# Attention value products of a small decoder trunk: from float32 products of one head each to split products of a head pair

## The chip, the cores and the metric

One core of one Trainium2 chip. The metric is the device time of one execution in microseconds; below it is the median of three runs. Five engines work side by side: TensorE (PE, matmuls; its weight loads are listed as PEld), VectorE (DVE), ScalarE (ACT), GpSimd (POOL) and SyncE (SP, which issues most transfers). Matmul results land in PSUM, eight banks of 512 float32 columns on 128 partitions; everything else lies in SBUF.

## The reference, cut to what matters

Two layers on a sequence of 256 tokens, width 1024, 16 heads of 64. Layer 0 has eight block-sparse heads and eight heads that attend to 64 keys selected by an indexer; layer 1 has sixteen dilated heads. At this length each head is a causal softmax with a bias, and then the product of the weights with the values:

```
p = jax.nn.softmax(logits, axis=-1).astype(v.dtype)
return (jnp.einsum('bhqnk,bhqnkd->bhqd', p_sel, v_sel)
        + jnp.einsum('bhqk,bhkd->bhqd', p_own, v_own))
...
x = x + mixed @ w_o[layer]
h = rmsnorm(x, ffn_norm[layer])
x = x + conv_ffn(h, w_up[layer], conv_w[layer], conv_b[layer], w_down[layer])
```

All is float32.

## The kernel before, in words

Nearly all products are made from exact parts: a float32 operand is split into a high part (a copy rounded to the type F32R by ACT) and a low part (operand minus high part, by DVE), and three products high x high, high x low, low x high are summed in PSUM (`mm3`, line 130). `split` (lines 121, 122) does this for a weight block of 128 x 1024 right before it is used; raw blocks have three buffers, parts have five.

Attention in either layer goes over four chunks of four heads. A chunk projects q and k (`proj_fm`, 256 columns each, result with features on partitions) and v (`proj_v`, result with tokens on partitions, evacuated by ACT on line 312 into the float32 tile V, which holds all 1024 value columns for both token tiles t = 0, 1). Then come two calls of `head_pair`, two heads s = 0, 1 each:

- `logits`: queries on partitions, keys in columns. Queries 0 to 127 see keys 0 to 127 (128 columns), queries 128 to 255 all 256, so a head has 384 columns (TW). Products on lines 357 and 358, into one of two PSUM banks "lg".
- DVE adds the bias and takes the minimum (line 375), ACT takes the exponential and its sum (378), DVE inverts the sums (380) and scales the 128 and the 256 columns (382).
- PE transposes the three 128-column blocks (385) into the one PSUM bank "pt", and ACT copies them to SBUF as float32 (387): keys 0 to 127 against 256 queries, then keys 128 to 255 against the last 128 queries.
- Value products are plain float32 products (lines 392 and 396): a head's 64 value columns are the stationary operand, so its result stands on 64 of the 128 partitions of the one PSUM bank "av", head 0 on the lower half, head 1 on the upper. The trace shows each float32 product as two records.
- ACT copies the result as high part `mxh` (397), DVE makes the low part `mxl` (398).

`out_proj` then sums the output projection over the eight pairs hp; pairs 0 to 4 may start early, 5 to 7 close each of the four PSUM banks in turn, after which a norm reads them and the FFN follows (up products line 130, tiles u; down products, tiles o). The last pair (hp 7) uses the banks in other roles.

In layer 0 DVE also selects keys between the projections: 16 rounds of maximum and replace on the scores (lines 696, 697), whose result `selb` is needed from head 8 on. POOL adds it to the bias there (lines 724, 725). The indexer runs ahead of the attention.

The order of instructions on every engine is fixed when the program is built: a planner goes by program order, priorities and estimated times, so products of the next chunk and of the output projection stand between those of a head pair. At run time each engine takes its instructions in that order. A tile with a tag shares its buffers with all tiles of that tag; a new one is written when the one before it in the buffer is no longer read.

## Time and profile before

| what | value |
|---|---|
| runs | 663.56, 663.67, 664.44 us; median 663.67 |
| profiled execution | 663.93 us, span from first to last instruction 662.1 us |
| granted TensorE clock | 0.997 of full |
| PE busy | 649.3 us, 98% of the span, 5145 products |
| DVE, ACT, POOL busy | 530.5, 406.2, 58.0 us (80%, 61%, 9%) |
| DMA | 116.01 MB, mean 175 GB/s |

Busy time is the time in which at least one instruction of an engine runs. Products on PE overlap in a pipeline, so what one costs is seen from the start of one to the start of the next, not from its duration. The share of an engine is a mean over stages: indexer to 66 us, layer 0's attention to 153 us, its FFN to 363 us, layer 1's attention to 458 us, and its FFN.

### The profile page before, as it was taken

What the parts mean: (1) busy time and instruction counts of PE and PEld (TensorE: products, weight loads), DVE (VectorE), ACT (ScalarE), POOL (GpSimd) and SP (SyncE); (2) the same over time, 40 slices, a digit from 0 to 9 for tenths busy, and PEclk for the clock granted to TensorE, in tenths of its full rate; (3) what the DMA queues carried; (4) which work ended last, traced back from release to release, by engine and by line L of the source; (5) the groups of instructions that cost most, each with busy time, mean ns of one, the idle gap of its engine ahead of it and who ended that gap; (6) DMA issues with size and microseconds to landing.
All of it is one profiled execution on the core that took longest, in us unless ns stands there. A gap on an engine that the chain in (4) does not pass through costs nothing.

```text
span 662.1 us, 12930 instructions
## 1 busy us (share of the span) xinstructions
PE 649.3 (98%) x5145; PEld 616.6 (93%) x5145; DVE 530.5 (80%) x1012; ACT 406.2 (61%) x710; POOL 58.0 (9%) x68
## 2 busy tenths in 40 slices
PE   8999999999999999999999999999999999999995
PEld 6999998988999999999989988999999999999994
DVE  5999998966898777777779977765999777777774
ACT  6766774765676555555546866764587555555553
POOL 0100001712100000000013111010300000000002
PEclk9999999999999999999999999999999999999998
DMA  9986644462766666666323534537366555555201
GB/s 272 292 243 188 174 137 153 157 220 98 247 216 207 208 207 207 207 207 207 128 65 128 192 101 155 191 128 256 117 184 227 195 186 185 184 185 187 105 1 63
DMA packets 91604, 116.01 MB, mean 175 GB/s; under 512 B 3447, under 2 KB 83191, under 8 KB 91544
## 3 DMA queue, kind: packets, MB, share of 16 engines
q1 hardware_dynamic: 86492, 110.09, 50.5%
q10 hardware_dynamic: 5052, 5.10, 3.3%
q8 instruction: 40, 0.66, 0.4%
q14 instruction: 20, 0.16, 0.1%
HBM read 113.35 MB, written 1.84 MB: 174 GB/s over the span
## 4 chain that ended last, share of the span: by engine, by line
PE 95%; DVE 2%; DMA 1%; issue 1%; SPq 0%; ACT 0%; POOL 0%; POOLq 0%; DVEq 0%
PE f0u L130 18%; PE f1u L130 18%; PE f1o L130 9%; PE f0o L130 9%; PE a0o L130 3%; PE a1o L130 3%; PE a0av L392 1%; PE a1av L392 1%; PE a_0pt L385 1%; PE v02p L130 1%; PE v11p L130 1%; PE v01p L130 1%; PE v12p L130 1%; PE v03p L130 1%; PE v13p L130 1%; PE k02p L130 1%
## 5 line engine op out<-in xcount | busy, mean ns | idle before, releaser
L130 PE MATMUL f0u<-f0xl,f0w_0h 128*128 128x256 f32 x176 | 49.5, 281 | 1.2 <-DVE f0xl L204 1.2
L130 PE MATMUL f1u<-f1xl,f1w_0h 128*128 128x256 f32 x176 | 49.5, 281 | 0.3
L130 PE MATMUL f0u<-f0xh,f0w_0l 128*128 128x256 f32 x176 | 49.2, 280 | 0.0
L130 PE MATMUL f1u<-f1xh,f1w_1h 128*128 128x256 f32 x176 | 49.2, 280 | 0.0
L130 PE MATMUL f0u<-f0xh,f0w_1l 128*128 128x256 f32 x176 | 49.1, 279 | 0.0
L130 PE MATMUL f1u<-f1xl,f1w_1h 128*128 128x256 f32 x176 | 49.1, 279 | 0.0
L130 PE MATMUL f1u<-f1xh,f1w_0l 128*128 128x256 f32 x176 | 49.1, 279 | 0.0
L130 PE MATMUL f0u<-f0xh,f0w_1h 128*128 128x256 f32 x176 | 49.1, 279 | 0.0
L130 PE MATMUL f0u<-f0xh,f0w_0h 128*128 128x256 f32 x176 | 49.1, 279 | 0.0
L130 PE MATMUL f0u<-f0xl,f0w_1h 128*128 128x256 f32 x176 | 49.1, 279 | 0.0
L130 PE MATMUL f1u<-f1xh,f1w_1l 128*128 128x256 f32 x176 | 49.1, 279 | 0.0
L130 PE MATMUL f1u<-f1xh,f1w_0h 128*128 128x256 f32 x176 | 49.1, 279 | 0.0
L523 DVE SCALAR_TENSOR_TENSOR f1c<-f1us,cv,f1c 128x255 f32<-128x255 f32 (+1 forms) x88 | 37.0, 475 | 0.7 <-ACT f1c L520 0.7
L523 DVE SCALAR_TENSOR_TENSOR f0c<-f0us,cv,f0c 128x255 f32<-128x255 f32 (+1 forms) x88 | 36.9, 476 | 0.0
L121 ACT ACTIVATE f1w_0h<-f1uv 128x1024 fp32r<-128x1024 f32 x22 | 23.2, 1056 | 21.9 <-PE f1u L130 21.9
L121 ACT ACTIVATE f0w_0h<-f0uv 128x1024 fp32r<-128x1024 f32 x22 | 23.3, 1057 | 21.8 <-PE f0u L130 21.5
L130 PEld LDWEIGHTS f0u<-f0xl,f0w_0h 128*128 128x128 f32 x176 | 33.1, 188 | 1.8 <-DVE f0xl L204 1.6
L130 PEld LDWEIGHTS f1u<-f1xl,f1w_0h 128*128 128x128 f32 x176 | 33.1, 188 | 1.6 <-DVE f1xl L204 0.8
L121 ACT ACTIVATE f0w_1h<-f0ug 128x1024 fp32r<-128x1024 f32 x22 | 23.3, 1059 | 17.4 <-PE f0o L130 12.2
L130 PEld LDWEIGHTS f1u<-f1xh,f1w_0h 128*128 128x128 f32 x176 | 33.1, 188 | 0.8
L130 PEld LDWEIGHTS f1u<-f1xh,f1w_0l 128*128 128x128 f32 x176 | 33.1, 188 | 0.0
L130 PEld LDWEIGHTS f1u<-f1xl,f1w_1h 128*128 128x128 f32 x176 | 33.1, 188 | 0.0
(1055 smaller groups left out, 2493.6 us busy)
## 6 DMA issues: line engine op xcount, KB each, us to landing
f0dn<-in_w_down_dram SPq DMA_DIRECT2D x11, 1024.0 KB, 5.0
f0uv<-in_w_up_dram SPq DMA_DIRECT2D x11, 1024.0 KB, 5.9
f0ug<-in_w_up_dram SPq DMA_DIRECT2D x11, 1024.0 KB, 5.0
f1dn<-in_w_down_dram SPq DMA_DIRECT2D x11, 1024.0 KB, 4.8
f1uv<-in_w_up_dram SPq DMA_DIRECT2D x11, 1024.0 KB, 6.7
f1ug<-in_w_up_dram SPq DMA_DIRECT2D x11, 1024.0 KB, 5.1
q<-in_w_in_even_dram SPq DMA_DIRECT2D x4, 1024.0 KB, 6.7
k<-in_w_in_even_dram SPq DMA_DIRECT2D x4, 1024.0 KB, 6.0
```

Source lines behind the costliest of these rows:

```text
L121: nc.scalar.activation(h, view, AF.Copy)
L130: m = nc.tensor.matmul(ps, w, a, start=start and i == 0, stop=stop and i == 2, **kw)
L385: nc.tensor.transpose(pt[:, c * P:(c + 1) * P], pr[:, c * P:(c + 1) * P], ident)
L392: nc.tensor.matmul(o[:, 0:S], V[:, 0, vc], pts[s][:, 0:S], start=True, stop=False)
L523: nc.vector.scalar_tensor_tensor(c[:, i, sh:S], u[:, i, 0:S - sh], cv[:, j, col:col + 1], c[:, i, sh:S], op0=ALU.mult, op1=ALU.add)
```

## The change

V is kept as a high and a low part (F32R), for two chunks at a time instead of four: ACT writes the high part as before, DVE the low part from the same PSUM tile. The normalised and transposed weights of a head pair are kept in the same way, in two tiles `pth` and `ptl` of 128 x (2 x 384), both heads side by side; ACT writes the high part, DVE the low. Of the two scalings with the inverse sums, the one of 256 columns moves from DVE to ACT. The value products are then three for each token tile: 128 value columns (both heads) stationary, the weights of both heads as 512 moving columns for t = 0 and 256 (two runs of 128) for t = 1. The result is 128 x 2 x 256: on each head's 64 partitions only that head's 256 columns are used. So the copies to `mxh` and `mxl` are made for each half of the partitions by itself. The weight tiles come from the pool that also holds the FFN's gated activations (tag "g2", five buffers, now 768 columns wide), and the tile `kiw` shares a buffer with a later constant.

```diff
--- before.py
+++ after.py
@@ -298,7 +298,7 @@
         evac(ps.rearrange("p (i c) -> p i c", i=2))
         return m
 
-    def proj_v(w2d, c0, xh, xl, r, v0, name, gate=None):
+    def proj_v(w2d, c0, xh, xl, r, V, name, gate=None):
         raw = load_cols(w2d, c0, name)
         hl = [split(raw[:, 4 * i:4 * i + 4, :], [4, 256], f"{name}_{i}", gate) for i in range(2)]
         ps = acc_tile(f"{name}p")
@@ -309,7 +309,9 @@
                 h, l = hl[k // 4]
                 mm3(o, h[:, k % 4, :], l[:, k % 4, :], xh[:, k, ts], xl[:, k, ts],
                     k == 0 and t == 0, k == KT - 1, swap=True, skip_group_check=True)
-            nc.scalar.activation(V[:, t, v0:v0 + 256], o, AF.Copy, scale=r[:, t:t + 1])
+            vh, vl = V[:, 0, t, :], V[:, 1, t, :]
+            nc.scalar.activation(vh, o, AF.Copy, scale=r[:, t:t + 1])
+            nc.vector.scalar_tensor_tensor(vl, o, r[:, t:t + 1], vh.bitcast(F32), op0=ALU.mult, op1=ALU.subtract)
 
 
 
@@ -359,8 +361,8 @@
         return lg
 
     def head_pair(hp, qs, ks, kl, bias, name):
-        av = (pt_tile if hp == 7 else av_tile)(f"{name}av{hp}")
-        pts = []
+        av = (pt_tile if hp == 7 else av_tile)(f"{name}av{hp}").rearrange("p (s c) -> p s c", s=2)
+        pth, ptl = (part_tile(f"{name}{hp}pt{i}").rearrange("p (s c) -> p s c", s=2) for i in "hl")
         for s in range(2):
             n = f"{name}{hp}_{s}"
             slot = 2 * (hp % 2) + s
@@ -378,24 +380,23 @@
                 nc.scalar.activation(pr[:, cols[t]], lb[:, cols[t]], AF.Exp, bias=nm[:, t:t + 1], scale=-1.0,
                                      accum_out=den[:, t:t + 1])
             nc.vector.reciprocal(den, den)
-            for t in range(2):
-                nc.vector.tensor_scalar(pr[:, cols[t]], pr[:, cols[t]], den[:, t:t + 1], None, op0=ALU.mult)
+            nc.vector.tensor_scalar(pr[:, cols[0]], pr[:, cols[0]], den[:, 0:1], None, op0=ALU.mult)
+            nc.scalar.activation(pr[:, cols[1]], pr[:, cols[1]], AF.Copy, scale=den[:, 1:2])
             pt = (lg_tile if hp == 7 else pt_tile)(n + "pt")
             for c in range(3):
                 nc.tensor.transpose(pt[:, c * P:(c + 1) * P], pr[:, c * P:(c + 1) * P], ident)
-            ptS = tp.tile([P, TW], F32, tag="ptS", name=n + "ptS", bufs=3)
-            nc.scalar.activation(ptS, pt[:, 0:TW], AF.Copy)
-            pts.append(ptS)
+            nc.scalar.activation(pth[:, s, :], pt[:, 0:TW], AF.Copy)
+            nc.vector.tensor_tensor(ptl[:, s, :], pt[:, 0:TW], pth[:, s, :].bitcast(F32), ALU.subtract)
+
+        vc = slice(hp % 2 * P, (hp % 2 + 1) * P)
+        for t, qc, o in ((0, slice(0, S), av), (1, slice(S, TW), av[:, :, P:S])):
+            for i, (v, p) in enumerate(((0, pth), (0, ptl), (1, pth))):
+                nc.tensor.matmul(o, V[:, hp // 2 % 2, v, t, vc], p[:, :, qc], start=t + i == 0, stop=t == 1 and i == 2,
+                                 skip_group_check=True)
         for s in range(2):
-            vc = slice((2 * hp + s) * HD, (2 * hp + s + 1) * HD)
-            o = av[s * HD:(s + 1) * HD, :]
-            nc.tensor.matmul(o[:, 0:S], V[:, 0, vc], pts[s][:, 0:S], start=True, stop=False)
-        for s in range(2):
-            vc = slice((2 * hp + s) * HD, (2 * hp + s + 1) * HD)
-            o = av[s * HD:(s + 1) * HD, :]
-            nc.tensor.matmul(o[:, P:S], V[:, 1, vc], pts[s][:, S:TW], start=False, stop=True)
-        nc.scalar.activation(mxh[:, hp, :], av[:, 0:S], AF.Copy)
-        nc.vector.tensor_tensor(mxl[:, hp, :], av[:, 0:S], mxh[:, hp, :].bitcast(F32), ALU.subtract)
+            own = slice(s * HD, (s + 1) * HD)
+            nc.scalar.activation(mxh[own, hp, :], av[own, s, :], AF.Copy)
+            nc.vector.tensor_tensor(mxl[own, hp, :], av[own, s, :], mxh[own, hp, :].bitcast(F32), ALU.subtract)
 
     def out_proj_start(name):
         return [acc_tile(f"{name}o{b}") for b in range(4)]
@@ -466,6 +467,9 @@
 
 
     LAG = 3
+
+    def part_tile(name):
+        return tp.tile([P, 2 * TW], F32R, tag="g2", name=name, bufs=LAG + 2)
 
     def ffn(layer, norm, name, nxt, also=None):
         xh, xl = norm.xh, norm.xl
@@ -525,8 +529,8 @@
             sg = tp.tile([P, S], F32, tag="sg", name=f"{name}sg{f}")
             nc.scalar.activation(sg, c[:, 1, :], AF.Silu)
             nc.vector.tensor_tensor(sg, sg, c[:, 0, :], ALU.mult)
-            g2 = tp.tile([P, 2, S], F32R, tag="g2", name=f"{name}g{f}", bufs=LAG + 2)
-            gh, gl = g2[:, 0, :], g2[:, 1, :]
+            g2 = part_tile(f"{name}g{f}")
+            gh, gl = g2[:, 0:S], g2[:, S:2 * S]
             high = nc.scalar.activation(gh, sg, AF.Copy)
             if also is not None:
                 also(f, high.ins)
@@ -600,7 +604,7 @@
         ss0s = tp.tile([P, 2], F32, tag="ss", name="ss0s")
         nc.vector.tensor_add(ss0s, ss0[:, :, 0], ss0[:, :, 1])
         r0 = rsqrt_mean(ss0s, D, "n0")
-    kiw = cp.tile([80, S], F32, tag="kiw", name="kiw")
+    kiw = cp.tile([80, S], F32, tag="cv", name="kiw")
     nc.scalar.activation(kiw, psk[0:80, 0:S], AF.Copy)
 
     score = cp.tile([P, TW], F32, tag="score", name="score")
@@ -616,7 +620,7 @@
     wq = cp.tile([P, 2, NH], F32, tag="wq", name="wq")
     jk = tp.tile([P, 2, HD], F32, tag="jk", name="jk", bufs=1)
     tp.tile([P, 16], F32, tag="gap", name="gap", bufs=1)
-    ki = tp.tile([P, 2, S], F32R, tag="g2", name="ki", bufs=LAG + 2)
+    ki = part_tile("ki")[:, 0:2 * S].rearrange("p (i c) -> p i c", i=2)
     trow = bias_rows(high.ins)
 
     def index_keys():
@@ -703,7 +707,7 @@
     selection = select()
 
     def attn_tiles(name):
-        return (cp.tile([P, 2, D], F32, tag="V", name=name + "V"),
+        return (cp.tile([P, 2, 2, 2, 256], F32R, tag="V", name=name + "V"),
                 cp.tile([P, 8, S], F32R, tag="mxh", name=name + "mxh"),
                 cp.tile([P, 8, S], F32R, tag="mxl", name=name + "mxl"))
 
@@ -732,7 +736,7 @@
         next(selection, None)
         proj_fm(we, base + 512, x0h, x0l, k_evac(ks, kl, rb0, f"k0{c}t"), f"k0{c}")
         next(selection, None)
-        proj_v(we, base + 1024, x0h, x0l, r0, 256 * c, f"v0{c}")
+        proj_v(we, base + 1024, x0h, x0l, r0, V[:, c % 2], f"v0{c}")
         head_pair(2 * c, qs, ks, kl, bias0, "a0")
         head_pair(2 * c + 1, qs, ks, kl, bias0, "a0")
     n = Norm(16, "f0")
@@ -758,7 +762,7 @@
         proj_fm(wo1, 256 * c, n1.xh, n1.xl, q_evac(qs, rb1, f"q1{c}t"), f"q1{c}")
         proj_fm(wo1, 1024 + 256 * c, n1.xh, n1.xl, k_evac(ks, kl, rb1, f"k1{c}t"), f"k1{c}",
                 (None, gate), (low, nc.vector))
-        proj_v(wo1, 2048 + 256 * c, n1.xh, n1.xl, r1, 256 * c, f"v1{c}", gate)
+        proj_v(wo1, 2048 + 256 * c, n1.xh, n1.xl, r1, V[:, c % 2], f"v1{c}", gate)
         for hp in (2 * c, 2 * c + 1):
             head_pair(hp, qs, ks, kl, lambda h: (nb1[:, h, P:S], nb1[:, h, :]), "a1")
     n = Norm(24, "f1")
```

## Rows read from the trace of the kernel before

**Rows 1.** The page: shares of the chain of work that ended last, by engine.

```profile
PE 95%; DVE 2%; DMA 1%; issue 1%; SPq 0%; ACT 0%; POOL 0%; POOLq 0%; DVEq 0%
```

**Rows 2.** Busy time by stretches: stretch, its length, each engine's busy us (instructions), clock, DMA.

```profile
66.00:100.00 34.00, 34.00 (x276) 31.51 (x275) 32.50 (x102) 25.17 (x59) 2.40 (x4) 1.00 0.55 161
...
66.00:118.00 52.00, 52.00 (x421) 48.14 (x420) 47.23 (x140) 34.23 (x72) 5.72 (x7) 1.00 0.51 158
118.00:132.00 14.00, 14.00 (x117) 13.06 (x116) 12.89 (x40) 9.92 (x27) 10.11 (x13) 1.00 0.45 152
132.00:153.40 21.40, 21.40 (x173) 19.07 (x171) 13.19 (x33) 12.24 (x30) 3.11 (x4) 1.00 0.57 197
...
363.00:458.20 95.20, 95.20 (x771) 88.02 (x770) 69.96 (x169) 64.11 (x139) 8.33 (x8) 1.00 0.50 169
```

**Rows 3.** PE's timeline, first burst of a pair: start, us, engine, line, operation.

```profile
98.85 0.28 PE L130 MATMUL v02p<-v_0h,n0xl 128*128 128x256 f32 x1
...
99.63 0.39 PE L130 MATMUL v02p<-v_0l,n0xh 128*128 128x256 f32 x1
99.86 0.28 PE L130 MATMUL v02p<-v_1h,n0xh 128*128 128x256 f32 x1
```

**Rows 4.** PE's timeline, second burst of another pair, with the plain products around it.

```profile
90.75 0.28 PE L130 MATMUL k02p<-n0xh,k_0h 128*128 128x256 f32 x1
...
92.50 0.28 PE L130 MATMUL k02p<-n0xh,k_0h 128*128 128x256 f32 x1
...
93.50 0.39 PE L130 MATMUL k02p<-n0xl,k_0h 128*128 128x256 f32 x1
93.73 0.27 PE L385 MATMUL a_0pt<-ident,a_0pr 128*128 128x128 f32 x1
```

**Rows 5.** PE's timeline in the second FFN: twelve products of 512 columns between these.

```profile
559.77 0.63 PE L130 MATMUL f1o<-f1d8h,f1g 128*128 128x512 f32 x2
...
562.57 0.28 PE L130 MATMUL f1u<-f1xh,f1w_0h 128*128 128x256 f32 x1
```

**Rows 6.** PE's timeline, 128-column products of one head's logits, and the next.

```profile
88.93 0.22 PE L357 MATMUL a_0lg<-a0qk 128*128 128x128 f32 x1
...
89.11 0.33 PE L357 MATMUL a_0lg<-a0qk 128*128 128x256 f32 x1
```

**Rows 7.** DVE's timeline in layer 0.

```profile
87.18 0.42 DVE L398 TENSOR_TENSOR a0mxl<-a0av,a0mxh 128x256 fp32r<-128x256 f32 x1
87.51 1.22 DVE L122 TENSOR_TENSOR v_1l<-v,v_1h 128x1024 fp32r<-128x1024 f32 x1
88.64 0.42 DVE L696 MAX8 m<-score 128x8 f32<-128x256 f32 x1
...
90.09 0.54 DVE L382 TENSOR_SCALAR a_0pr<-a_0pr,a_0den 128x128 f32<-128x128 f32 x2
90.54 0.54 DVE L382 TENSOR_SCALAR a_1pr<-a_1pr,a_1den 128x128 f32<-128x128 f32 x2
...
93.68 1.40 DVE L329 TENSOR_TENSOR a0qk<-q02t,a0qk 64x512 fp32r<-64x512 f32 x2
...
130.07 1.22 DVE L122 TENSOR_TENSOR a0wo3l<-a0wo,a0wo3h 128x1024 fp32r<-128x1024 f32 x1 [1.01 <-ACT a0wo3h L121]
```

**Rows 8.** All engines' timeline at layer 0's end; last row the chain at layer 1's end.

```profile
153.44 0.38 ACT L397 ACTIVATE a0mxh<-a0av 128x256 fp32r<-128x256 f32 x1 [2.22 <-PE a0av L396]
...
153.88 0.38 PE L130 MATMUL a0o<-a0mxh,a0wo7h 128*128 128x256 f32 x1
...
458.15 7.33 PE a1o L130 x61
```

**Rows 9.** The chain in order of time: transposes of two neighbouring heads.

```profile
84.56 0.48 PE a_0pt L385 x3
...
88.42 0.33 PE a_1pt L385 x3
```

**Rows 10.** Line 312: evacuations of chunk 2's V, durations, first and last start.

```profile
L312 ACT ACTIVATE a0V<-v02p,n0r x2: 452/464/477, 103.1 to 110.4; 128x256 f32<-128x256 f32 x2
```

## The prediction

> **What bounds the kernel now.** I read the core's span and clock first: 662.1 us at a granted clock of 0.997, the fast one of TensorE's two levels (2.4 GHz), so nothing is to be won or lost there. Then the chain that ended last [rows 1]: 95% of it is TensorE (PE). Then busy time by stretches [rows 2]. Both attention stretches (66 to 153.4 us in layer 0, 363 to 458.2 us in layer 1) show a PE with no idle time at all; projections of the next chunk and output products fill every gap between the attention products. The reader should see two things in these rows: time taken off PE there is time taken off the kernel as long as the others keep up, and VectorE (DVE) has little left in layer 0: 47.23 of 52 us from 66 to 118, 12.89 of 14 to 132, against 13.19 of 21.4 afterwards and 69.96 of 95.2 in layer 1. ScalarE (ACT) has 44.2 of 66 us in the first two. So I then read PE's timeline around the changed products, and DVE's for the price of an instruction.
>
> **PE: what the value products cost today.** A plain 128x256 product of the split type takes 0.117 us from start to start (15 of them between 90.75 and 92.50 in [rows 4]). In [rows 3] the first burst of a pair (one head's 256 columns) sits between two plain products: 98.85 to 99.86 is 1.01 us, two plain slots are 0.23, so the burst costs 0.78. In [rows 4] the second burst (other head's 256, both heads' 128) takes 92.50 to 93.73, 1.23 us less two slots, 1.00. Where transposes follow at once a little less is lost, so I take 1.75 us a pair, and 16 pairs (8 in each layer) make 28.0 us.
>
> **PE: what they will cost.** Three products of 128 by 512 and three of 128 by 256, all of the split type. Twelve such 512-column products take 559.77 to 562.57 in [rows 5], 0.233 us each; 256 columns 0.117. So 3 x 0.233 + 3 x 0.117 = 1.05 us a pair, 16.8 us in all. The half of each result that is thrown away is in these columns. PE's saving is 28.0 - 16.8 = 11.2 us, 0.70 a pair. No row shows a 256-column product whose columns lie in two runs of 128, as the last three have. Below, it costs as a contiguous one, 0.117; above, as two 128-column products, 0.18 by [rows 6] (88.93 to 89.11) up to 0.233 if each half pays a full slot. That is 0 to 3 x 0.116 x 16 = 5.6 us. I take 0, because the runs are long, and keep 5.6 for the range.
>
> **DVE: what is added.** Prices are start to start, since neighbours overlap. A 128x256 subtraction from PSUM holds DVE 0.33 us (87.18 to 87.51 in [rows 7]), a 128x1024 one 1.13 (87.51 to 88.64), so 128 more elements cost about 0.13, and a 384-wide subtraction 0.47. A scaling pair of 128 and 256 columns holds it 0.45 (90.09 to 90.54), of which I give 0.26 to the 256. Halving the partitions saves nothing: 64x512 takes 0.70 each in [rows 7], and 512 on the slope from 0.42 (256) to 1.22 (1024) would be 0.69. Per pair then: two low parts of the weights +0.94, a second half of the output's low part +0.34, two scalings moved to ACT -0.52: +0.76; and each of the two low parts of V in a chunk +0.34, one per pair. In all +1.10 a pair, 8.8 us a layer.
>
> In layer 1 that makes 69.96 + 8.8 = 78.8 of 95.2 - 5.6 = 89.6 us, 88%. From 66 to 100 us DVE stands at 32.50 of 34, 96%, and PE still never waits [rows 2]; so I charge layer 1 nothing. In layer 0, from 66 to 132, five pairs' value products and six evacuations of V are done: 5 x 0.76 + 6 x 0.34 = 5.8 us more, 47.23 + 12.89 + 5.8 = 65.9 us of DVE where PE would want 66 - 3.5 = 62.5. DVE is short by 3.4 us. Part can go later: four splits of the output weights (the 1.13 us kind; the fourth, a0wo3l, starts at 130.07 in [rows 7]) lie before 132, and after 132 DVE has 8 us free. But they feed the products that fill PE. Bounds: 0 if all 3.4 us is put off, 5.5 if nothing is and queues add 2 us. I take 2.0.
>
> A rule bears on that term. In a sentence of its own: the Trainium skill, "SBUF — State Buffer", section Who interferes with whom, says that DVE's scalings can enter a mode that locks out GpSimd, while an instruction with one SBUF input does not; the new subtractions have one (the other is in PSUM). By it the moved scalings free more in layer 0, where GpSimd works, than I count; a saving of up to 1 us would make the sum 1 us lower. No row isolates this, and the 2.0 stands without it.
>
> **ACT, buffers, tails.** ACT gets two 256-column scalings and a second half of the output's high part, at 0.38 to 0.5 us each [rows 8] some 1.3 us a pair: about 7 us on 44.2 of 66, hidden by ACT's own idle time; without that cover they would lengthen the softmax chain, which PE's filler covers. The copy of the transposed weights is only renamed. V kept for two chunks means chunk 2 may not write before chunk 0's last product: those are over by 93.5 us [rows 4], the write starts at 103.1 [rows 10]; cost nothing, 9.6 us of cover. Two weight tiles a pair out of five buffers hold two and a half pairs; cost nothing while not more than two are in flight. At the end of layer 0 PE already waits for the last copy (153.44 ACT, 153.88 PE [rows 8]); with two half copies in a row it waits 0.38 us longer, if the low halves keep up. The longer way to the last product (subtraction 0.47, a late hop to ACT) lies in the 2 us in which PE runs output products before it. In layer 1, 7.33 us of output products follow the last pair's without a wait [rows 8], so I charge it nothing. Term: +0.4, up to +1.6 if each layer pays 0.8.
>
> For that tail, again by itself: the Trainium skill, "PSUM — Partial Sum Buffer", section on bank collisions, says that engines reading one bank must take turns unless they are in different quadrants. By it the second high half and the first low half, on other partitions, can run together, as my 0.4 has it; taking turns by whole bank would make it 0.8 a layer, and the sum 1.2 higher. No row has two halves.
>
> **Sum.** The profiled execution took 663.93 us: 663.93 - 11.2 + 2.0 + 0.4 = 655.1. The median shown is 0.26 lower than that execution, so 654.9; I say 655.
>
> **Rivals.**
> *PE's saving lands whole* (0.20): selection and weight splits of layer 0 move behind 132 us. For it, the 8 us free there [rows 2]; against it, the products that those splits feed. 663.7 - 11.2 = 652.5, 651.5 if the old bursts also delayed their neighbours.
> *DVE eats layer 0* (0.12): the 3.4 us shortfall cannot move, and its queue adds 2. Layer 0 then gains nothing, layer 1 its 5.6, less tails: 659 to 660.
> *Slower: the transposes' PSUM bank* (0.10). There is one; until now it is free after ACT's copy, then only after DVE's subtraction, which stands in DVE's queue behind splits of 1.13 us. If the next head's transposes, and PE behind them in its fixed order, wait more than 11.2 / 32 = 0.35 us a head, the gain is gone; at 0.55, one subtraction, it is 32 x 0.55 = 17.6 - 11.2, 6.4 us slower, 670. Against it: transposes of neighbouring heads start 3.9 us apart in [rows 9], and the bank is held some 1.5 to 2.7.
> *The strided products don't run at full rate* (0.05): the 5.6 us above, 660.5.
>
> **How the numbers follow.** The forecast holds 0.53. 651.5 to 661.5 takes in the first two rivals, the third and the strided price; it leaves out the slower one, and sums in which several bounds meet. A measurement here tells 0.2% (1.3 us) from no change: faster is below 662.3. The forecast and the first rival are all faster (0.73), of the DVE and strided cases 0.12; the other 0.05 of those two is no change, and the bank rival is slower (0.10). So faster 0.85, same 0.05, slower 0.10.
>
> **What would show it.** After: per pair six value products, 512 columns 0.233 us apart and 256 ones 0.117, with plain products next to them at plain spacing. Some 5.6 us off the stretch of layer 1, 3 off layer 0's. DVE over 97% busy from 66 to 132 us, with the first idle time of PE there, ended by DVE. PE waiting some 0.4 us longer for the last copies of layer 0. The prediction is wrong if transposes are seen waiting for the weights' subtraction, if the strided products lie over 0.18 apart, or if PE idles in layer 1.

## The result, and the profile after

The changed kernel takes 669.58 us (median of 4 runs, 667.76 to 671.11) against 664.06 (663.56 to 664.67) for the kernel before in the same series: a ratio of 1.0086, interval 1.0067 to 1.0105. It is slower by 5.5 us where 655 was forecast. Its profiled execution has a span of 667.0 us (before 662.1) at a mean clock of 0.990 (0.997); in all four executions the mean clock is 0.989 or 0.990. As an estimate, (0.997 - 0.990) x 667 = 4.7 us of the loss are time at the lower clock.

The page after, shares of the chain that ended last by engine:

```profile
PE 89%; DVE 6%; DMA 2%; issue 1%; ACT 1%; SPq 0%; POOL 0%; POOLq 0%; DVEq 0%; ACTq 0%
```

PE had 95% in [rows 1]; VectorE and a transfer have taken its place somewhere. Where, the busy time by stretches tells (columns as in [rows 2]):

```profile
66.00:118.00 52.00, 52.00 (x439) 51.59 (x438) 51.28 (x144) 39.40 (x84) 4.43 (x6) 1.00 0.54 163
118.00:132.00 14.00, 14.00 (x120) 13.86 (x118) 12.23 (x41) 10.22 (x30) 9.04 (x13) 1.00 0.38 138
132.00:153.40 21.40, 17.42 (x117) 16.00 (x116) 15.54 (x41) 14.87 (x37) 3.32 (x4) 0.87 0.60 197
153.40:160.00 6.60, 6.39 (x44) 5.82 (x43) 2.25 (x5) 2.00 (x5) 0.00 (x0) 0.90 0.32 117
...
367.00:455.00 88.00, 88.00 (x739) 87.18 (x738) 75.63 (x179) 70.84 (x157) 8.66 (x8) 1.00 0.49 164
455.00:460.00 5.00, 3.41 (x27) 3.04 (x25) 2.00 (x3) 1.78 (x3) 0.00 (x0) 1.00 1.07 350
460.00:465.00 5.00, 3.62 (x13) 3.12 (x14) 2.86 (x5) 1.85 (x6) 0.00 (x0) 0.69 0.06 11
```

Up to 118 us PE is full, as before, and has more records behind it (439 against 421), although its value products have advanced less: three pairs with 18 of these records, against four pairs with 32. It has done filler, the products of the next chunk and of the output projection, ahead of the pairs. Then two holes open, one at the end of each attention: 4.2 us of PE's time idle between 132 and 160 us (0.05 in the kernel before), 3.0 between 455 and 465, and the granted clock is lower in or behind them (0.87 to 0.90, and 0.69). DVE is 99% busy up to 118 us (51.28 of 52), not the 47.23 of [rows 2], but only about half busy in the second hole (4.86 of 10 us).

PE's own price is the forecast one. PE's own timeline, with no row left out from 123.17 on:

```profile
122.36 0.39 PE L394 MATMUL a0av<-a03pth,a0V 128*128 128x512 f32 x1
122.59 0.28 PE L130 MATMUL a0o<-a0mxh,a0wo1l 128*128 128x256 f32 x1
...
123.17 0.28 PE L130 MATMUL a0o<-a0mxl,a0wo1h 128*128 128x256 f32 x1
123.29 0.40 PE L394 MATMUL a0av<-a03ptl,a0V 128*128 128x512 f32 x1
123.53 0.51 PE L394 MATMUL a0av<-a03pth,a0V 128*128 128x512 f32 x2
123.87 0.28 PE L394 MATMUL a0av<-a03ptl,a0V 128*128 128x256 f32 x1
123.99 0.28 PE L394 MATMUL a0av<-a03pth,a0V 128*128 128x256 f32 x1
124.11 0.28 PE L130 MATMUL a0o<-a0mxh,a0wo1l 128*128 128x256 f32 x1
```

The first of the six stands apart and takes 0.23 us from start to start (122.36 to 122.59). The other five take 0.82 (123.29 to 124.11; the row x2 holds one of 512 and one of 256 columns); the strided 256 columns are 0.12 apart, and the plain product behind them comes 0.12 later. Together that is 1.05 us a pair, as forecast, and 0.70 less than the bursts of [rows 3, 4]. DVE's added work is right in size too: 547.9 us busy after, 530.5 before, +17.4 where 2 x 8.8 were counted.

The table gives the stages of all traces that the text needs, in us from the span's start: the first product of layer 0's attention (q00p), when DVE's selection ends (start of the last instruction that writes `selb`), first product of layer 1 (q10p), first product of layer 1's FFN (f1u). Layer 0 is the time from the first of these products to the second (it takes in layer 0's FFN), layer 1 that from the second to the third. The attention begins between 35.2 and 36.6 us whatever the edit, so layer 0 is compared by its length and not by its end. The stages of a row come from one execution.

| kernel | attention begins | selection ends | layer 1 begins | its FFN begins | layer 0 | layer 1 | time, us | ratio to before (95%) |
|---|---|---|---|---|---|---|---|---|
| before | 35.8 | 116.4 | 349.0 | 466.8 | 313.2 | 117.8 | 664.06 | |
| after | 36.4 | 121.1 | 353.1 | 471.3 | 316.7 | 118.2 | 669.58 | 1.0086 (1.0067 to 1.0105) |
| no_weight_low | 35.2 | 109.3 | 345.7 | 460.0 | 310.5 | 114.3 | 657.96 | 0.991 (0.9894 to 0.9927) |
| before_extra_sub | 36.6 | 123.5 | 354.6 | 474.0 | 318.0 | 119.4 | 669.77 | 1.0091 (1.0073 to 1.0109) |
| half_selection | 35.4 | 98.8 | 347.6 | 466.7 | 312.2 | 119.1 | 664.2 | 1.0005 (0.9988 to 1.0023) |
| before_half_selection | 35.2 | 97.8 | 349.6 | 467.4 | 314.4 | 117.8 | 665.57 | 1.0036 (1.0024 to 1.0047) |
| ffn_split_behind | 35.9 | 120.3 | 352.8 | 466.7 | 316.9 | 113.9 | 663.76 | 0.9995 (0.9985 to 1.0006) |
| l0_second_behind | 36.3 | 121.0 | 352.4 | 466.4 | 316.1 | 114.0 | 664.34 | 1.0011 (1.0002 to 1.002) |
| wo_low_pool | 35.9 | 120.6 | 352.3 | 467.4 | 316.4 | 115.1 | 663.54 | 0.9995 (0.9982 to 1.0009) |
| pt_free_early | 35.7 | 122.1 | 352.6 | 466.9 | 316.9 | 114.3 | 665.08 | 1.0011 (0.9999 to 1.0023) |
| copies_grouped | 35.5 | 119.7 | 352.7 | 469.5 | 317.2 | 116.8 | 666.82 | 1.0044 (1.0031 to 1.0058) |
| no_lows_l1_behind | 35.2 | 108.8 | 345.9 | 459.9 | 310.7 | 114.0 | 656.86 | 0.989 (0.9868 to 0.9911) |
| no_lows_half_sel | 35.3 | 88.9 | 346.9 | 460.9 | 311.6 | 114.0 | 658.25 | 0.992 (0.9899 to 0.994) |
| v_pool_both_behind | 35.2 | 109.7 | 348.0 | 462.0 | 312.8 | 114.0 | 660.10 | 0.9954 (0.994 to 0.9968) |

So of the 4.9 us in the span, layer 0 brings 3.5 and layer 1 0.4, where -3.2 and -5.6 were forecast; 0.6 lie ahead of the attention and 0.4 behind layer 1's first FFN product.

### The profile page after: what moved, and what is told of

The parts are those of the page before. It is cut to its first block, busy times and chain, and to the rows that moved or that the text cites. A ratio compares the mean times of both kernels' runs of the same rounds, so it can differ in the third digit from the quotient of the medians.

```text
span 667.0 us, 12907 instructions
## 1 busy us (share of the span) xinstructions
PE 645.3 (97%) x5113; PEld 623.3 (93%) x5113; DVE 547.9 (82%) x1044; ACT 425.5 (64%) x758; POOL 56.2 (8%) x68
## 4 chain that ended last, share of the span: by engine, by line
PE 89%; DVE 6%; DMA 2%; issue 1%; ACT 1%; SPq 0%; POOL 0%; POOLq 0%; DVEq 0%; ACTq 0%
PE f0u L130 18%; PE f1u L130 18%; PE f1o L130 9%; PE f0o L130 9%; PE a0o L130 2%; PE a1o L130 2%; PE a1av L394 1%; PE a0av L394 1%; DMA f1ug<-in_w_up_dram 1%; DMA xtok<-in_x_dram 1%; DVE xT L219 1%; PE qi1p L130 1%; PE q03p L130 1%; PE q00p L130 1%; PE v01p L130 1%
## 5 line engine op out<-in xcount | busy, mean ns | idle before, releaser
L121 ACT ACTIVATE f1w_1h<-f1ug 128x1024 fp32r<-128x1024 f32 x22 | 23.3, 1061 | 19.8 <-DMA f1ug<-in_w_up_dram 10.8
```

The source lines that it names most:

```text
L121: nc.scalar.activation(h, view, AF.Copy)
```

## The experiments

The theory after the result: DVE's added work makes something late, and PE, which has done its filler sooner, runs dry at the end of each attention. The first rival: the one PSUM bank of the transposes, held until the low part is made. Edits are against the changed kernel unless said otherwise.

**The weights' low part left out: no_weight_low.** The second product reads `pth` again.

```diff
-            nc.vector.tensor_tensor(ptl[:, s, :], pt[:, 0:TW], pth[:, s, :].bitcast(F32), ALU.subtract)
-            for i, (v, p) in enumerate(((0, pth), (0, ptl), (1, pth))):
+            for i, (v, p) in enumerate(((0, pth), (0, pth), (1, pth))):
```

> The changed kernel without the subtractions that make the low part of the attention weights; the second value product reads the high part a second time, so TensorE has the same six products per pair. The result lacks the correction by the low part. It takes 0.47 us of VectorE per head away, 15 us in all. Theory A (VectorE's added work makes the last pairs of each layer late): 655 to 659 us, both holes near the end of the attentions mostly gone. Theory B (not VectorE's amount but the place of the weight splits in the queues ahead of the last pairs' copies): 663 to 668 us, the hole before the second FFN still there because its split still stands ahead of the last pair and waits for its load. Theory C (the new products or the longer hold of the banks cost TensorE its gain): as the changed kernel, 667 to 671.

657.96 us, 11.6 under the changed kernel with the same products on PE. This one DVE instruction a head is the whole loss and more, but it is both DVE time and bank time.

**The same work in the kernel before: before_extra_sub.** Its 128x384 subtraction goes to a tile that nobody reads.

```diff
             pts.append(ptS)
+            nc.vector.tensor_tensor(pr, pt[:, 0:TW], ptS, ALU.subtract)
```

> The kernel before with one more 128x384 subtraction from PSUM per head on VectorE (its result is not used): the added VectorE work and the longer hold of the transposes' bank, without the new products. Theory A (VectorE's amount): 4 to 9 us slower, 668 to 673. Theory B (place of the splits in the queues): within 2 us of the kernel before, since TensorE is then not ahead of the copies. Theory C (bank hold): TensorE waits for the bank at the transposes, some 0.3 us a head, 10 us slower.

669.77 us: 5.7 us slower with PE's products untouched. So DVE's room was not free in the kernel before either, though its PE never waited [rows 2]. This subtraction too takes DVE time and holds the bank; the run does not part the two.

**Bank or DVE: pt_free_early.** ACT copies the transposed weights once more to SBUF, DVE subtracts from there, and the bank is free after ACT.

```diff
-            nc.vector.tensor_tensor(ptl[:, s, :], pt[:, 0:TW], pth[:, s, :].bitcast(F32), ALU.subtract)
+            nc.scalar.activation(pr, pt[:, 0:TW], AF.Copy)
+            nc.vector.tensor_tensor(ptl[:, s, :], pr, pth[:, s, :].bitcast(F32), ALU.subtract)
```

> The changed kernel; ScalarE copies the transposed weights a second time, to SBUF, and VectorE makes the low part from that copy, so the transposes' PSUM bank is free after two ScalarE copies and no longer waits for VectorE's queue. VectorE's count stays, ScalarE gets 0.4 us a head, 13 us in all. Rival of the prediction (the bank's hold makes the kernel slower): 660 to 665. Theory A (VectorE's amount): no gain, 667 to 672.

In the changed kernel's timeline the second head's transposes start 6.2 us after the first's; the subtraction that frees the bank is over only at 80.94, 2.8 us after ACT's copy:

```profile
76.93 0.49 PE L387 MATMUL a_0pt<-ident,a_0pr 128*128 128x128 f32 x3
...
77.62 0.48 ACT L388 ACTIVATE a00pth<-a_0pt 128x384 fp32r<-128x384 f32 x1
...
80.39 0.55 DVE L389 TENSOR_TENSOR a00ptl<-a_0pt,a00pth 128x384 fp32r<-128x384 f32 x1
...
83.10 0.49 PE L387 MATMUL a_1pt<-ident,a_1pr 128*128 128x128 f32 x3
```

With the bank free early they start 3.9 us apart, as in [rows 9]:

```profile
76.22 0.49 PE L387 MATMUL a_0pt<-ident,a_0pr 128*128 128x128 f32 x3
...
80.09 0.49 PE L387 MATMUL a_1pt<-ident,a_1pr 128*128 128x128 f32 x3
```

So the bank does stretch the pitch. Up to 132 us that costs nothing, for PE has other products meanwhile. Layer 1 gains 3.9 us by the edit, layer 0 nothing (316.9 us after 316.7). But this does not clear the bank in layer 0. In the changed kernel the longest single wait of PE there, 2.10 of the 4.2 us, is one of transposes for the subtraction that frees their bank. The chain that ended last and PE's timeline show it:

```profile
139.07 1.14 DVE a0wo7l L122
140.21 0.24 issue
140.46 0.54 DVE a05ptl L389
```

```profile
141.05 0.90 PE L387 MATMUL a_1pt<-ident,a_1pr 128*128 128x128 f32 x3 [2.10 <-DVE a05ptl L389]
```

The subtraction stands in DVE's queue behind the splits of three output weights (a0wo5l to a0wo7l, from 136.71 on). In pt_free_early PE waits at the same place 0.88 and 1.81 us for ACT's second copy, which frees the bank there. The edit gives the bank to another late engine, so it can't tell what the hold costs layer 0; the next runs leave the hold as it is and take DVE's work away.

**Layer 0, the selection's end: half_selection and before_half_selection.** Half of the 16 rounds are left out, in the changed kernel and in the one before.

```diff
-            for i in range(TOPK // 8):
+            for i in range(TOPK // 16):
```

> Leaves out half of the 16 rounds of maximum and replace in layer 0's selection (so the selected keys differ), some 6.5 us of DVE's work ahead of selb. If DVE's load up to the selection's end is what costs layer 0 its gain: selb some 8 to 11 us earlier than 121.1, layer 1 starts at 347 to 349.5 instead of 353.1, layer 1 unchanged near 118, time 663.5 to 666. Rival, the transposes' one bank held by the subtraction: a wait per head that does not know the selection; layer 1 starts at 352 or later, time 668.5 to 670.

> The kernel before with the same half of the selection left out. DVE theory: its PE has no idle time in layer 0, so nothing is gained, 663 to 665, layer 1 starts at 348.3 to 349.5. Rival (the selection set layer 0's end already before): 661 or less.

Busy time of a stretch in half_selection, and the groups of `selb` and of layer 1's first products there (durations, first and last start):

```profile
132.00:153.40 21.40, 18.98 (x142) 17.29 (x141) 15.28 (x31) 15.01 (x35) 0.00 (x0) 1.00 0.63 207
```

```profile
L704 DVE TENSOR_SCALAR selb<-score x2: 203/240/278, 84.7 to 98.8; 128x256 f32<-128x256 f32 x1, 128x128 f32<-128x128 f32 x1
```

```profile
L130 PE MATMUL q10p<-n1xh,q_0h x8: 277/278/281, 347.6 to 353.8; 128*128 128x256 f32 x8
```

Layer 0 takes 312.2 us instead of 316.7, and layer 1 no less (119.1). PE idles 2.4 us between 132 and 153.4 instead of 4.0, and the clock is 1.00 there instead of 0.87. The same cut in the kernel before brings nothing: 665.57 us, 0.36% slower, and 314.4 us for layer 0 instead of 313.2. That separates the two: the kernel before was not bound by DVE's work in layer 0, the changed one is, with the subtraction on the bank left in place. How much of it goes by the selection itself, and how much by the weight splits that stand behind it in the queue, stays open: of two runs below with the selection over at 110.0 and 109.7, one gains 1.6 us in layer 0, the other, with a split of the FFN moved too, 3.9.

**Layer 1, the split in the queue: ffn_split_behind.** The first splits of either FFN wait in ACT's and DVE's order until the last pair's copies are issued.

```diff
-            nc.scalar.activation(mxh[own, hp, :], av[own, s, :], AF.Copy)
-            nc.vector.tensor_tensor(mxl[own, hp, :], ...)
+            done_h = nc.scalar.activation(mxh[own, hp, :], av[own, s, :], AF.Copy)
+            done = (done_h, nc.vector.tensor_tensor(mxl[own, hp, :], ...))
...
+    n.first_gate = done
...
-                        norm.gate if 1 <= f < 4 else None) for i in range(2)]
+                        norm.gate if 1 <= f < 4 else norm.first_gate if f == 0 else None) for i in range(2)]
```

> The changed kernel; only the two splits of the FFN's first weight block are queued, on ScalarE and VectorE, behind the copies of the attention's last pair. No work is added or removed. Theory B: 661 to 665 us, 3 to 6 us less than the changed kernel in the same run, the 3.2 us in which ScalarE waited for the load before the last copy gone in layer 1. Theory A or C: within 1.5 us of the changed kernel.

The timeline of the changed kernel at layer 1's end, rows of ACT and DVE:

```profile
451.41 1.23 DVE L122 TENSOR_TENSOR a1wo5l<-a1wo,a1wo5h 128x1024 fp32r<-128x1024 f32 x1
...
459.04 1.06 ACT L121 ACTIVATE f1w_1h<-f1ug 128x1024 fp32r<-128x1024 f32 x1 [3.22 <-DMA f1ug<-in_w_up_dram]
460.00 0.47 ACT L388 ACTIVATE a17pth<-a_1pt 128x384 fp32r<-128x384 f32 x1
...
460.13 1.23 DVE L122 TENSOR_TENSOR f1w_1l<-f1ug,f1w_1h 128x1024 fp32r<-128x1024 f32 x1 [3.10 <-ACT f1w_1h L121]
...
461.27 0.55 DVE L389 TENSOR_TENSOR a17ptl<-a_1pt,a17pth 128x384 fp32r<-128x384 f32 x1
```

and the issues of that transfer (first and last start):

```profile
L94 SPq DMA_DIRECT2D f1ug<-in_w_up_dram x11: 367/368/372, 452.7 to 617.7; - x11
```

Read it backwards. The last head's weights can be copied only at 460.00, though their transposes were done at 457.6, because ACT stands at 459.04 in a weight split that waits 3.22 us for a transfer. The transfer was issued at 452.66, 0.02 us after `a1wo5l` had read the raw buffer that it fills, and that split is 4.9 us later than before (446.5, issue at 447.7). In the kernel before the split came at 458.50, just behind the last copy. With the splits behind, the last head's weights are copied at once and the split comes last:

```profile
457.35 0.49 ACT L388 ACTIVATE a17pth<-a_1pt 128x384 fp32r<-128x384 f32 x1 [2.75 <-PE a_1pt L387]
...
461.83 1.04 ACT L121 ACTIVATE f1w_1h<-f1ug 128x1024 fp32r<-128x1024 f32 x1
```

Layer 1 takes 113.9 us instead of 118.2. The pairs themselves are no sooner: the split `a1wo5l` comes 98.3 us after layer 1's begin in both, as it did in the kernel before (97.5). PE's saving lies in output products that it has done ahead, and it becomes time only if nothing late stands at the end. Layer 0 gains nothing (316.9 us): its FFN's first product comes 3.5 us earlier (160.2 against 163.7), but then PE waits 2.3 us instead of 1.2 for the norm's `f0xl`, and from 166 to 172 the granted clock is 0.73. l0_second_behind, with only the second split of layer 0 behind, takes 316.1 there and 664.34 us in all, no better than with both behind, where 1 to 3 us less were expected.

> The changed kernel with the first FFN splits of layer 1, and of layer 0 the second one alone, queued behind the attention's last pair. Theory B for layer 0 too: the FFN's split no longer stands ahead of the last copies there, and the norm is not held up by two splits as it was with both behind: 660 to 663, 1 to 3 us less than with both behind in both layers. Theory A alone in layer 0: as with both behind, 663 to 665.

Three different edits, the splits behind, the bank free early and the low part left out, all bring layer 1 to 113.9 to 114.3, which points to one lateness, mended in three ways.

**DVE's load taken to other engines.** wo_low_pool gives low parts of the output weights to POOL (all of layer 1, pairs 4 to 7 of layer 0); v_pool_l1_behind the low parts of the v weights of layer 0's chunks 1 to 3, with layer 1's FFN splits behind; before_v_pool the same low parts in the kernel before; scale_on_dve takes the 256-column scaling back to DVE.

```diff
-        proj_v(we, base + 1024, x0h, x0l, r0, V[:, c % 2], f"v0{c}")
+        proj_v(we, base + 1024, x0h, x0l, r0, V[:, c % 2], f"v0{c}", None, nc.gpsimd if c else nc.vector)
```

> The changed kernel; the low parts of the output weights are made on GpSimd: all eight in layer 1, the last four in layer 0. VectorE loses 12 x 1.13 = 13.6 us, GpSimd gains some 12 x 2.4 = 28 us. Theory A (VectorE's amount): 657 to 662 us. Theory B: 663 to 669, since the FFN's split keeps its place and its load still waits for the output weights' buffer, now freed by a slower engine. Theory C: as the changed kernel.

> The changed kernel with two moves: in layer 0, chunks 1 to 3, the low parts of the weights of v (six splits) are made on GpSimd, which is idle there, and in layer 1 alone the first FFN splits are queued behind the last pair's copies. Theory A for layer 0 (VectorE paces it from 66 to 132 us) and B for layer 1 (a split that waits for its load stands ahead of the last copies): layer 0 gets 4 to 6 us shorter than in the changed kernel, layer 1 about 4, 657 to 660 us in all, below the kernel before. Rival (layer 0's hole is made by the output weights' splits alone, not by VectorE's amount): layer 0 unchanged, 663 to 665.

> The kernel before with the same six splits of v on GpSimd in layer 0. If VectorE already shared the pace of layer 0 before, and PE is full, relief can bring nothing: Theory A with PE as the bound of the kernel before: within 1.5 us of it, 662 to 665. Rival (the kernel before was held by VectorE too): 658 to 661.

> The changed kernel with the scaling of the 256 columns back on VectorE: 0.26 us more of VectorE per head, 4.2 us a layer, and as much less on ScalarE. Theory A: layer 0 2 to 4 us longer than in the changed kernel, 670 to 674 in all. Rival (ScalarE's added work and the hop to it make the pairs late): 664 to 667.

wo_low_pool takes 663.54 us, most of the gain from layer 1 (115.1); layer 0 keeps 316.4, so its late output weights alone are not the cause. v_pool_l1_behind takes 662.68 (0.9983, 0.9972 to 0.9994), with the selection over at 110.0 and layer 1 from 350.6. Layer 0 gains 1.6 us (315.1), not the 4 to 6 expected. In the kernel before the same move costs some 1.7 us by the ratio (665.51; 1.0026, 1.0012 to 1.004), though its selection ends 10 us earlier: DVE time taken away is worth something only since the change. scale_on_dve takes 670.41 (1.0098, 1.0072 to 1.0125), in all no measurable difference from the change. By stages layer 0 takes 3.2 us more (319.9), inside the 2 to 4 of Theory A, and layer 1 takes 1.3 less (116.9). One trace each does not settle the layers, but it agrees with DVE's load as layer 0's cost.

**Both cures: v_pool_both_behind** (V's low parts on POOL in layer 0, splits behind as in l0_second_behind), and v_wo_pool_both_behind with layer 0's late output weights on POOL as well.

> As the run before it, and six low parts of v's weights on GpSimd in layer 0. If the two causes add up: 657 to 661. If GpSimd's share of the memory ports lengthens VectorE's other work as much as it relieves it: as without, 661 to 663.

> As the run before it, and the low parts of layer 0's last four output weights on GpSimd as well (4.5 us less of VectorE between 130 and 146 us, where VectorE holds the copies of the fifth pair behind them). If the place of those splits makes the hole: 655 to 659. If not: as the run before.

660.10 and 660.09 us (the second 0.9949, 0.9936 to 0.9961): by the ratios some 3 us faster than the kernel before, and some 9 faster than the changed one. The second is no better than the first, so layer 0's late output weights on POOL add nothing.

**A third cure on top: v_pool_pt_free** adds pt_free_early's copy to v_pool_both_behind.

> V's low parts on POOL in layer 0 for chunks 1 to 3, the FFN's first split behind the last pair, and the transposed weights copied once more so that their bank comes free early. If bank hold and DVE's load are two separate costs, their gains (some 4.5 and 9.5 us) add in part: 656 to 658. If they are one cost (DVE too late at the layers' ends), the bank edit adds nothing to 660.1: 659.5 to 661.

668.16 us (1.0069, 1.0054 to 1.0084), some 8 slower than without it, and neither expectation. Its timeline, and then the group of the first such subtraction:

```profile
85.99 2.37 POOL L122 TENSOR_TENSOR v_0l<-v,v_0h 128x1024 fp32r<-128x1024 f32 x1 [7.78 <-ACT v_0h L121]
...
86.30 2.47 DVE L390 TENSOR_TENSOR a00ptl<-a_1pr,a00pth 128x384 fp32r<-128x384 f32 x1
...
112.43 2.40 POOL L122 TENSOR_TENSOR v_0l<-v,v_0h 128x1024 fp32r<-128x1024 f32 x1 [5.73 <-ACT v_0h L121]
112.51 2.73 DVE L390 TENSOR_TENSOR a03ptl<-a_0pr,a03pth 128x384 fp32r<-128x384 f32 x1
```

```profile
L390 DVE TENSOR_TENSOR a00ptl<-a_0pr,a00pth x1: 558/558/558, 81.2 to 81.2; 128x384 fp32r<-128x384 f32 x1
```

The subtraction now has both inputs in SBUF and is over only 0.41 us after POOL's: 2.47 and 2.73 us where it takes 0.56 alone. The selection ends at 116.6 instead of 109.7, and layer 1 begins at 356.9.

**How much is left: no_lows_l1_behind and no_lows_half_sel.** Without any low part of weights and V (the products read the high parts), splits behind; the second also with half the selection.

> The changed kernel without the subtractions for the low parts of both the weights and V (each product still runs, reading the high parts instead), and with the first FFN splits of layer 1 behind the last pair. The result lacks those corrections. VectorE then has 0.2 us a pair less than before the change. If TensorE's gain of 11 us is there to be had: 652 to 655 us. Rival (other parts of the change, the split copies and the buffers, keep some of it): 656 to 659.

> Leaves out the low parts of the weights and of V (the products read the high parts instead) and half of the selection's rounds, with the FFN's first split behind the last pair in layer 1 and its second in layer 0. Only PE's cheaper products are left of the change. If all of the missing gain was DVE's: 653 to 654.5, that is 10 to 11 us under the kernel before. If some 4 us of PE's saving are lost at the layers' ends whatever DVE does: 656 to 657.5, as without the low parts alone.

656.86 and 658.25 us: by the ratios 7.3 and 5.3 us under the kernel before, not 11; half of the selection less brings nothing more. In no_lows_half_sel the copy behind layer 0's last value product starts at 148.68, 4.8 us earlier than in [rows 8]. Around it PE runs dry:

```profile
146.00:150.00 4.00, 2.67 (x21) 2.33 (x19) 0.46 (x2) 0.81 (x3) 0.00 (x0) 1.00 0.23 34
...
160.00:166.00 6.00, 6.00 (x40) 6.00 (x41) 5.49 (x6) 2.89 (x4) 3.17 (x3) 0.73 0.36 119
```

The output products that filled the last pair's wait are done by then. 4.8 us early (0.5 of it because the attention begins sooner) has become 3.9 at the FFN's first product (155.7 against 159.6) and, after a stretch at clock 0.73, 2.1 at layer 1's first.

**The half copies: copies_grouped**, both high halves written ahead of both low ones, and v_pool_behind_grouped, the same on v_pool_both_behind.

```diff
+        for s, own in enumerate(owns):
+            nc.scalar.activation(mxh[own, hp, :], ...)
+        for s, own in enumerate(owns):
+            nc.vector.tensor_tensor(mxl[own, hp, :], ...)
```

> The changed kernel with both high half copies of a pair's result written ahead of both low ones. In the changed kernel ACT's second half always starts right after DVE's first subtraction (149.09 to 149.13, 155.29 to 157.88 for two pairs). If that is an order between the instructions, given by the order in which they are written (the second copy writes a tile whose other half is being read), the last high half comes 0.4 us earlier and the last low half 0.4 to 0.8, at each layer's end: 667.5 to 669, up to 2 us better if pairs in between gain too. Rival: engines take turns at the bank of the result, whatever the order written; ACT's second half still waits for DVE or DVE's first waits for ACT's second, and the time stays at 669 to 670.

> The same grouping on the version with V's low parts on POOL in layer 0 and the FFN's first split behind the last pair (660.1). There the last pairs' halves run in series from 149.90 to 153.05 at layer 0's end with the FFN's second split behind them. Order as written: 658.5 to 659.7. Turns at the bank: 660 to 660.6.

In the changed kernel the four copies of a pair run one after the other, ACT's second half only when DVE's first is done:

```profile
463.78 0.38 ACT L398 ACTIVATE a1mxh<-a1av 64x256 fp32r<-64x256 f32 x1 [1.22 <-PE a1av L394]
464.19 0.42 DVE L399 TENSOR_TENSOR a1mxl<-a1av,a1mxh 64x256 fp32r<-64x256 f32 x1 [1.17 <-ACT a1mxh L398]
464.64 0.38 ACT L398 ACTIVATE a1mxh<-a1av 64x256 fp32r<-64x256 f32 x1 [0.48 <-DVE a1mxl L399]
465.05 0.43 DVE L399 TENSOR_TENSOR a1mxl<-a1av,a1mxh 64x256 fp32r<-64x256 f32 x1 [0.44 <-ACT a1mxh L398]
```

Grouped, DVE's first waits for ACT's second:

```profile
153.40 0.77 ACT L398 ACTIVATE a0mxh<-a0av 64x256 fp32r<-64x256 f32 x2 [1.13 <-PE a0av L394]
154.20 0.86 DVE L400 TENSOR_TENSOR a0mxl<-a0av,a0mxh 64x256 fp32r<-64x256 f32 x2 [1.34 <-ACT a0mxh L398]
```

666.82 us, some 2.8 better than the change by the two ratios, and 660.17 (0.9947, 0.9935 to 0.996), no better than without. The last high half is there 0.77 us after the first began instead of 1.24, the last low half no earlier. The 2.8 us are more than this; other instructions changed places too (layer 0's `f0w_1h` starts 3.4 us earlier), so they are not all the copies'. Nor are the holes smaller in layer 0: PE idles 4.6 us between 132 and 160 (4.2 in the changed kernel), but the clock is 1.00 there and between 455 and 465, where the changed kernel had 0.87, 0.90 and 0.69. A gain of 2.8 us may lie in the clock alone. Whether the order between the engines comes from the written order or from the shared bank stays open: in neither kernel do they overlap.

## Why the prediction was wrong

- **PE's saving of 11.2 us: right as a price.** 0.70 us a pair, strided products at full rate; that rival is out. But a saving on PE counts only where PE has something else to do. At the end of an attention it has not: even without the low parts' DVE work 5.3 to 7.3 us are gained. The prediction itself had seen that the gaps are filled by output products; it didn't ask what is left to fill with when PE is 5 us sooner.
- **"I take 2.0" for DVE in layer 0: the step that failed first.** The shortfall of 3.4 us was worked out rightly, but treated as work that can partly be put off, with 5.5 as its bound. It could not be: the selection stands in the same queue, its end moved from 116.4 to 121.1, and four pairs wait for it; behind it come the splits of the output weights, ahead of the late pairs' copies. Layer 0 came out at +3.5 us, so beside PE's -5.6 and the tail's +0.4 the term measured 8.7, not 2.0. Of the 9.1 us between -5.6 and +3.5, PE's idle 4.2 are not quite half. The lower clock is up to (1 - 0.87) x 21.4 + (1 - 0.90) x 6.6 = 3.4 us, an estimate from the rows above; the prediction had no term for it. The remaining 1.5 stay unexplained. half_selection returns 4.5 of the 9.1, at a clock of 1.00.
- **"I charge layer 1 nothing": the step that failed second.** It argued from a busy share of 88%, and from PE never waiting at 96%. The busy share was about right, and DVE has room in the hole (4.86 of 10 us busy, and 3.10 us of waiting for that same split). What it did not follow was the queue: a layer that begins 4.1 us later, a raw buffer free 4.9 us later, a transfer 4.9 us later, and a split waiting for it ahead of the last head's copies. Idle 3.0 us and up to (1 - 0.69) x 5 = 1.6 of clock are 4.6 of the 6.0 us that layer 1 misses; the splits behind return 4.3. The trace of before gave no sign of it: there the split (458.50) stood behind ACT's last copy (458.19), and its transfer, issued at 447.7, had some 5 us in hand (the transfers of `f1ug` land 5.0 to 5.6 us after issue). The change altered the planned order as well as the times: the split now stands ahead of the last head's copies.
- **The tail, +0.4 up to 1.6: mis-sized.** The forecast let the second high half run beside the first low half; they take turns, and the last high half is ready 0.86 us after the first (464.16 to 465.02), not 0.38. The Trainium skill, "PSUM — Partial Sum Buffer", section on bank collisions, allows access in different quadrants at the same time; no run here shows such an overlap.
- **The rival "transposes' PSUM bank"** had the right sign and a real wait (pitch 6.2 instead of 3.9 us), and was put at 0.10. Its mechanism, a wait of PE each head, is not the one: PE is full until 132 us. But the sign that the prediction set for being wrong, transposes waiting for the weights' subtraction, was seen once, and it is half of layer 0's hole (2.10 of 4.2 us). What made that subtraction late is DVE's queue: half_selection returns 4.5 us with the bank held as before, while freeing the bank with ACT returns nothing in layer 0. So its 670 us, so near to 669.58, is luck. In layer 1 the bank is one of three ways to the same lateness.
- **"DVE eats layer 0"** named the place and stopped at no gain there, 659 to 660, because it took DVE's shortfall and 2 us of queue for the whole cost and layer 1 for safe.

Open: what the remaining 4 to 6 us at the layers' ends would need (more filler for PE, or a shorter chain from the last selection to the norm), since no run here supplied either; and why the clock fell behind some holes and not behind others.

## What to carry to other kernels

Before you count a saving on the busiest engine, look at the end of each stage, list what it still has to fill with and which chain ends last there, and shorten that chain too. Work added to an engine at 90% or more is not priced by its busy time but by what stands last in its queue (here the selection), and by who is freed later because of it (a buffer, a transfer, a split ahead of the copies). An instruction that waits for a transfer belongs behind the last urgent one in its queue: that took 4.3 us off layer 1. And compare stages by their lengths, with the clock beside them: a start 1 us earlier or a clock of 0.87 in one stretch is as large as the effects looked for.

## What the runs showed of the hardware

- Beside a POOL subtraction, a DVE subtraction with both inputs in SBUF ended only 0.41 to 0.42 us after POOL's, three times: 2.47, 2.58 and 2.73 us instead of 0.56 (v_pool_pt_free). The Trainium skill, "SBUF — State Buffer", section Who interferes with whom, says that such an instruction contends with a GpSimd instruction that reads SBUF, and one with at most one SBUF input, outside the modes that use both ports, doesn't. The traces agree: in v_pool_both_behind the same subtraction reads PSUM and takes 0.56 us (108.47 to 109.03) inside a POOL subtraction (107.19 to 109.61), and the selection ends at 109.7 us instead of 116.6.
- A hole of 3 to 4 us in PE's work cost, by the estimates above, up to half as much to nearly as much again: the granted clock of the stretches with or after it was 0.87, 0.90, 0.69 and 0.73, a mixture of the two levels (2.4 and 1.2 GHz), and 1.00 in the stretches ahead of it. It was not so each time: with 4.6 us idle between 132 and 160 (copies_grouped) and with 3.4 (before_extra_sub) the clock was 1.00 there.
- POOL takes 2.37 to 2.45 us for the 128x1024 subtraction for which DVE takes 1.22.
